# First weight pair of a split feed-forward block: all products with the first tokens before those with the second, its sums on one engine, and out rows joined with norms

## Chip, cores and metric

One core of a Trainium2 chip runs the whole kernel. The metric is device time in microseconds (us), as the median of several runs. A profile of one execution comes beside it. Engines are TensorE (PE: matrix products and transposes), VectorE (DVE), ScalarE (ACT), GpSimd (POOL) and SyncE (SP, which only issues DMAs). Each engine works through its own queue in order; across engines they wait on semaphores.

## The reference, cut to what matters

```python
x = x + 0.5 * swiglu(x, ffn1_norm, w_gate1, w_up1, w_down1)
...                      # windowed attention and latent attention on rms(x)
x = x + concat(rms(o_a), rms(o_b)) @ w_out
x = x + 0.5 * swiglu(x, ffn2_norm, w_gate2, w_up2, w_down2)

def swiglu(x, g, w_gate, w_up, w_down):
    h = rms(x, g)        # x * rsqrt(mean(x*x) + 1e-6) * g
    return (silu(h @ w_gate) * (h @ w_up)) @ w_down
```

x is 1024 tokens by 1024 features in float32; the hidden width is 2816, that is 22 tiles of 128.

## The kernel before, in words

Every float32 product is made from three products of rounded parts: an operand is split into `hi` (rounded by ACT, line 99 or, in `unit`, 358) and `lo` (the rest, subtracted by DVE, line 100 or 359), and `products` issues hi x hi, hi x lo and lo x hi (lines 120, 121, 122). A weight or activation is thus usable only when ACT and then DVE have treated it.

`ffn` runs twice, for the first and the last line of the reference. Its normed rows (`ys`, by `norm_rows`) are turned on PE (`bank`, line 226) and put as hi and lo into four blocks (`Block.put`, lines 212 and 213): B11 and B21 hold the two feature halves of the first 512 tokens, B12 and B22 those of the last 512. From the second hidden tile pair on, gate and up are made by a fast scheme with seven products in place of eight: it needs sums of the activation blocks (T1 to T4, made once by the generator `sums`, lines 235 to 255: `whole` adds hi and lo again, the rest subtracts) and sums S1 to S4 of each weight pair (`make`, line 295, called through `prepare`, which runs `AHEAD` = 5 products ahead). The first pair of hidden tiles (`f` = 0, 1, each with gate `wg` and up `wu`) is made plainly, while T1 to T4 are made: `half_unit(w, th)` multiplies one weight tile with the tokens of one half (`th`), 24 matmuls of 512 columns. So the first stage has eight half units: gate and up, two tiles, two halves. `finish` (lines 339 to 352) multiplies silu(gate) with up, writes it out on POOL's DMA queue and forms four sums of a finished pair.

Before the second `ffn`, `out_rows(1, t)` makes the second half of w_out's product for 128 tokens (24 matmuls; line 1212 adds it to x on DVE), the row is normed, and POOL's queue writes it to `x2`.

What sets the order of the work is a scheduler that takes the program as it is written and interleaves it per engine; which buffer becomes free when is set by pools (45 `slot`, 12 `tmp`, 8 PSUM banks).

Of the kernel before, what the change touches and what calls it, by code (L numbers as in the profile page):

```python
# [10 lines left out]
F32 = mybir.dt.float32  # L11
F32R = mybir.dt.float32r
AF = mybir.ActivationFunctionType
ALU = mybir.AluOpType
# [4 lines left out]
P = 128  # L19
# [40 lines left out]
def tile_layer(ctx: ExitStack, tc: tile.TileContext, x, g1n, mixn, g2n, wg1, wu1, wd1, wg2, wu2, wd2,  # L60
# [154 lines left out]
        def hi_lo(self, k):  # L215
            return tuple(self.t[hl][k // 2][:, k % 2, :] for hl in range(2))

    def ffn(rows_in, ys, gain, wg, wu, wd, act_d, xsrc, done, aside=iter(())):


        y = {}
# [6 lines left out]

        B11, B12, B21, B22, T1, T2, T3, T4 = (Block() for _ in range(8))

        def whole(blk, k, eng):

            d = tmp([P, 512])
            hi, lo = blk.hi_lo(k)
            eng.tensor_tensor(d, hi.bitcast(F32), lo.bitcast(F32), op=ALU.add)
            return d

        def turned(blk, th, k):
# [2 lines left out]

        def sums():
            for k in range(4):
                b12 = whole(B12, k, nc.gpsimd)
                t1 = whole(B11, k, nc.vector)
                nc.vector.tensor_tensor(t1, b12, t1, op=ALU.subtract)
                T1.put(k, t1)
                yield
                t3 = whole(B22, k, nc.gpsimd)
                nc.vector.tensor_tensor(t1, t3, t1, op=ALU.subtract)  # L250
                nc.vector.tensor_tensor(t3, t3, b12, op=ALU.subtract)
                T3.put(k, t3)
                yield
                t4 = whole(B21, k, nc.gpsimd)
                nc.gpsimd.tensor_tensor(t4, t4, t1, op=ALU.subtract)
                T2.put(k, t1)
                yield
                T4.put(k, t4)
                yield
# [25 lines left out]
        def make(c, nme, which):  # L285
            if which == "M11":
                load_pair(*((c, "u") if nme == "g" else (c + 1, "g")))
            f1, f2 = raws[(c, nme)]
            m = {"M11": f1[:, :512], "M12": f1[:, 512:], "M21": f2[:, :512], "M22": f2[:, 512:]}
            need = {"S1": ("M21", "M22", ALU.add), "S2": ("S1", "M11", ALU.subtract),  # L290
                    "S3": ("M11", "M21", ALU.subtract), "S4": ("M12", "S2", ALU.subtract)}
            if which in need:
                a_, b_, op = need[which]
                src = tmp([P, 512])
                nc.gpsimd.tensor_tensor(src, sums_[a_] if a_ in sums_ else m[a_], sums_[b_] if b_ in sums_ else m[b_],
                                        op=op)
# [33 lines left out]
        def finish(f, th, gate, up):  # L330
# [24 lines left out]
        def unit(raw, eng):  # L355
            hi, lo = slot([P, 1024], F32R), slot([P, 1024], F32R)
            for c in (slice(0, 512), slice(512, 1024)):
                nc.scalar.activation(hi[:, c], raw[:, c], AF.Copy)  # L358
                eng.tensor_tensor(lo[:, c], raw[:, c], hi[:, c].bitcast(F32), op=ALU.subtract)  # L359
# [12 lines left out]
        w0 = unit(first[0], nc.vector)  # L372
        for blk in (B11, B21):
            for k in range(4):
                turned(blk, 0, k)
        gen2 = sums()
        for f in range(2):
            for th in range(2):
                pts = []
                for i in range(2):  # L380
                    pts.append(half_unit(w1 if i else w0, th))
                    if f == 0 and th == 0 and i == 1:
                        for k in range(4):
                            turned(B12, 1, k)
                        for k in range(4):
                            turned(B22, 1, k)
                    if f == 0 and th == 0 and i == 0:
                        w1 = unit(first[1], nc.gpsimd)
                        for t in range(4, 8):
                            y[t] = ys(t)  # L390
                    if (f, th) > (0, 0):
                        for _ in range(3):
                            next(gen2, None)
                    if f == 0 and th == 1:
                        if i == 0:
                            n0 = unit(second[0], nc.vector)
                        else:
                            n1 = unit(second[1], nc.vector)
                    if f == 1 and th == 0 and i == 0:
                        load_pair(1, "g")  # L400
                    if f == 1 and th == 1:
                        prepare(1 + i)
                sg = tmp([P, 512])
                nc.scalar.activation(sg, pts[0], AF.Silu)
                finish(f, th, sg, pts[1])
            w0, w1 = (n0, n1) if f == 0 else (None, None)
            first = second = None if f else second
        for _ in gen2:
            pass
        B12.t = None  # L410


# [229 lines left out]

        defer(2 if t < 4 else 4, turn)

    ffn(load_rows, lambda t: norm_rows(x0.pop(t), both=True), g1n, wg1, wu1, wd1, act_d, x, mid, rel_bias_rows())


    def project(hT, ws, width, sink, ahead, last):
# [643 lines left out]

    ffn(lambda t: None, lambda t: normed[t], g2n, wg2, wu2, wd2, act_d, x2, fin)
    flush()


# [74 lines left out]
```

## Time and profile before

| | |
|---|---|
| median of 3 runs | 1884.24 us (1882.35 to 1884.5) |
| profiled execution | 1881.59 us, its span 1879.8 us |
| PE busy | 1825.7 us, 97% |
| DVE, ACT, POOL busy | 1271.2, 775.4, 627.8 us |
| mean granted clock of PE | 0.993 of full |

The span runs from the first to the last instruction. A page of the profile gives busy time by engine, by line and in slices; a timeline gives the rows in order of time as "start, duration, engine, line, operation, output <- inputs, count", with the idle time before a row and what ended it in brackets. The first `ffn` fills the span up to some 650 us, the second begins at 1221 us.

### The profile page before, as it was taken

To read this page: it belongs to the slowest core of one execution; us is meant where nothing else is said; L and a number is where in the kernel's file an instruction comes from. 1 tells how busy PE (TensorE), PEld (TensorE's weight loads), DVE (VectorE), ACT (ScalarE), POOL (GpSimd) and SP (SyncE) were. 2 spreads that over 40 slices of the span, in tenths; PEclk is the share of its full clock that TensorE was granted. 3 is DMA by queue.
4 is the path that set the end of the run, shared out by engine and by line. 5 is a ranking of instruction groups with operands and counts; after the bars stand their busy time and mean duration, and the time that the engine had idled before them with its cause. 6 is when DMAs were issued, how large, how long until landed. Compare 5 with 4: busy or idle time off the path is not lost.

```text
span 1879.8 us, 25149 instructions
## 1 busy us (share of the span) xinstructions
PE 1825.7 (97%) x9088; PEld 1546.2 (82%) x9088; DVE 1271.2 (68%) x2127; ACT 775.4 (41%) x1782; POOL 627.8 (33%) x706
## 2 busy tenths in 40 slices
PE   7899999999999999999998999979999999999998
PEld 5688888888888888888998888868888888888887
DVE  7976766766968363337888683388676767678681
ACT  5333333334445242236876582243333333253550
POOL 5643455442000122332454521256445444510000
PEclk9899999999999999999999999989999999999999
DMA  4223243326943231123311232313224222397422
GB/s 179 79 90 109 95 142 122 102 78 244 343 140 107 96 128 34 34 69 112 91 37 29 57 114 78 124 56 107 96 84 135 96 99 92 105 337 269 123 62 90
DMA packets 87078, 215.50 MB, mean 115 GB/s; under 512 B 11847, under 2 KB 17689, under 8 KB 86953
## 3 DMA queue, kind: packets, MB, share of 16 engines
q1 hardware_dynamic: 69608, 154.54, 25.0%
q0 software_dynamic: 17344, 59.35, 9.3%
q8 instruction: 71, 1.16, 0.2%
q14 instruction: 55, 0.44, 0.1%
HBM read 150.32 MB, written 59.33 MB: 112 GB/s over the span
## 4 chain that ended last, share of the span: by engine, by line
PE 88%; DVE 7%; issue 2%; DMA 1%; ACT 1%; POOL 1%; SPq 0%; POOLq 0%; DVEq 0%
PE ps L122 19%; PE ps L120 19%; PE ps L121 19%; PE ps L469 7%; PE ps L468 7%; PE ps L467 7%; PE ps L781 2%; DVE slot L100 2%; PE ps L807 2%; PE ps L755 1%; PE ps L846 1%; PE ps L771 1%; PE ps L969 1%; DVE slot L213 1%; PE ps L173 1%
## 5 line engine op out<-in xcount | busy, mean ns | idle before, releaser
L120 PE MATMUL ps<-slot,slot 128*128 128x512 f32 (+3 forms) x1728 | 664.3, 386 | 8.3 <-ACT slot L358 5.4
L122 PE MATMUL ps<-slot,slot 128*128 128x512 f32 (+3 forms) x1728 | 655.2, 383 | 14.4 <-DVE slot L359 13.1
L121 PE MATMUL ps<-slot,slot 128*128 128x512 f32 (+3 forms) x1728 | 661.5, 383 | 0.0
L122 PEld LDWEIGHTS ps<-slot,slot 128*128 128x128 f32 x1728 | 326.0, 189 | 78.3 <-DVE slot L359 14.0
L120 PEld LDWEIGHTS ps<-slot,slot 128*128 128x128 f32 x1728 | 325.8, 189 | 72.8 <-ACT slot L358 6.2
L121 PEld LDWEIGHTS ps<-slot,slot 128*128 128x128 f32 x1728 | 325.9, 189 | 62.3 <-DVE slot L213 0.5
L100 DVE TENSOR_TENSOR slot<-tmp,slot 128x512 fp32r<-128x512 f32 x346 | 332.5, 963 | 61.1 <-ACT slot L99 61.1
L99 ACT ACTIVATE slot<-tmp 128x512 fp32r<-128x512 f32 x346 | 215.2, 625 | 201.9 <-PE ps L469 43.6
L100 DVE TENSOR_TENSOR slot<-slot,slot 128x512 fp32r<-128x512 f32 (+3 forms) x312 | 254.2, 825 | 25.1 <-ACT slot L99 23.7
L468 PE MATMUL ps<-slot,slot 128*128 128x512 f32 x616 | 239.9, 390 | 0.0
L469 PE MATMUL ps<-slot,slot 128*128 128x512 f32 x616 | 239.7, 389 | 0.0
L467 PE MATMUL ps<-slot,slot 128*128 128x512 f32 x616 | 237.3, 389 | 0.0
L99 ACT ACTIVATE slot<-slot 128x512 fp32r<-128x512 f32 (+3 forms) x312 | 195.5, 641 | 61.0 <-PE ps L469 39.0
L468 PEld LDWEIGHTS ps<-slot,slot 128*128 128x128 f32 x616 | 115.6, 188 | 24.1
L469 PEld LDWEIGHTS ps<-slot,slot 128*128 128x128 f32 x616 | 115.6, 188 | 24.0
L467 PEld LDWEIGHTS ps<-slot,slot 128*128 128x128 f32 x616 | 115.6, 188 | 23.8
L543 ACT ACTIVATE tmp<-tmp 128x512 f32<-128x512 f32 x80 | 50.0, 625 | 199.6 <-DVE tmp L536 108.4
L528 DVE TENSOR_TENSOR tmp<-tmp,ps 128x512 f32<-128x512 f32 x40 | 27.5, 687 | 153.3 <-ACT tmp L527 153.3
L527 ACT ACTIVATE tmp<-ps 128x512 f32<-128x512 f32 x40 | 23.9, 597 | 226.1 <-PE ps L122 226.1
L342 POOL DMA_DIRECT2D act<-slot x22 | 16.2, 734 | 252.1 <-DVE slot L339 252.1
L475 DVE SCALAR_TENSOR_TENSOR slot<-ps,slot 128x512 f32<-128x512 f32 x56 | 36.9, 685 | 79.6 <-PE ps L469 79.5
L763 ACT ACTIVATE slot<-slot,tmp 128x256 f32<-128x256 f32 (+1 forms) x128 | 59.8, 468 | 22.4 <-DVE tmp L756 21.9
(174 smaller groups left out, 2278.2 us busy)
## 6 DMA issues: line engine op xcount, KB each, us to landing
tmp<-act SPq DMA_DIRECT2D x154, 256.0 KB
act<-slot POOLq DMA_DIRECT2D x66, 512.0 KB, 4.3
slot<-in_wg_dram SPq DMA_DIRECT2D x44, 512.0 KB
slot<-in_wu_dram SPq DMA_DIRECT2D x44, 512.0 KB
slot<-in_wd_dram SPq DMA_DIRECT2D x40, 512.0 KB
slot<-in_x_dram SPq DMA_DIRECT2D x16, 512.0 KB
x_mid<-slot POOLq DMA_DIRECT2D x16, 512.0 KB, 3.0
slot<-x_mid SPq DMA_DIRECT2D x16, 512.0 KB
```

The source lines that it names most:

```text
L99: nc.scalar.activation(hi, src, AF.Copy)
L100: nc.vector.tensor_tensor(lo, src, hi.bitcast(F32), op=ALU.subtract)
L120: nc.tensor.matmul(pt, ah, bh, start=first and i == 0, stop=False, skip_group_check=not first)
L121: nc.tensor.matmul(pt, ah, bl, start=False, stop=False, skip_group_check=not first)
L122: nc.tensor.matmul(pt, al, bh, start=False, stop=i == total - 1, skip_group_check=not first)
L467: nc.tensor.matmul(banks[i], ah, w[:, 0, :], start=first and k == 0, stop=False, skip_group_check=not first)
L468: nc.tensor.matmul(banks[i], ah, w[:, 1, :], start=False, stop=False, skip_group_check=not first)
L469: nc.tensor.matmul(banks[i], al, w[:, 0, :], start=False, stop=k == KD - 1, skip_group_check=not first)
L543: nc.scalar.activation(q, q, AF.Silu)
L763: nc.scalar.activation(self.p[:, e, :w], self.p[:, e, :w], AF.Exp, bias=self.m[e], scale=-1.0, accum_out=self.den[e])
L781: nc.tensor.matmul(po[:, e * HD:(e + 1) * HD], self.pt[:, n * P:(n + 1) * P], self.head["values"](self.far, self.j, e, j - nb + 1), start= ...
L807: nc.tensor.matmul(pt[:, :max(w, 256)], a, b, start=i == 0, stop=i == len(mats) - 1)
```

## The change

The loops over `f` (hidden tile) and `th` (token half) of the first stage are exchanged: all four half units with the first tokens are made first, then the four with the second. For that, four weight tiles are split and kept, and they are loaded before the rows of tokens 4 to 7. `sums` is advanced by four steps behind each half unit of the second tokens, instead of three behind each half unit from the third on. All additions that POOL made in `whole`, `sums`, `make`, `finish` and `unit` are on DVE. A new argument `lead` says how many rows of the second half are prepared ahead of the first half unit. In the second block (`lead` = 2) `out_rows`, `norm_rows` and the write to `x2` of a row group stand together in `last_rows`, which `ffn` calls, so that the out rows of groups 6 and 7 come behind the first half unit in the program.

```diff
         def sums():
             for k in range(4):
-                b12 = whole(B12, k, nc.gpsimd)
-                t1 = whole(B11, k, nc.vector)
+                t1, b12 = whole(B11, k), whole(B12, k)
 ...
-                t4 = whole(B21, k, nc.gpsimd)
-                nc.gpsimd.tensor_tensor(t4, t4, t1, op=ALU.subtract)
+                t4 = whole(B21, k)
+                nc.vector.tensor_tensor(t4, t4, t1, op=ALU.subtract)
@@ make
-                nc.gpsimd.tensor_tensor(src, sums_[a_] ...
+                nc.vector.tensor_tensor(src, sums_[a_] ...
@@ finish
-                nc.gpsimd.tensor_tensor(s43[:, 1, :], a11, a21, op=ALU.subtract)
-                nc.gpsimd.tensor_tensor(s43[:, 0, :], a12, s12[:, 1, :], op=ALU.subtract)
+                nc.vector.tensor_tensor(s43[:, 1, :], a11, a21, op=ALU.subtract)
+                nc.vector.tensor_tensor(s43[:, 0, :], a12, s12[:, 1, :], op=ALU.subtract)
@@ the first stage
-        first = [raw_of(wg[0]), raw_of(wu[0])]
+        raw = [raw_of(w[f]) for f in range(2) for w in (wg, wu)]
         for t in range(4, 8):
             rows_in(t)
-        second = [raw_of(wg[1]), raw_of(wu[1])]
-        for t in range(4):
+        for t in range(4 + lead):
             y[t] = ys(t)
 ...
-        for f in range(2):
-            for th in range(2):
+        for th in range(2):
+            for f in range(2):
                 pts = []
                 for i in range(2):
+                    n = 2 * f + i
+                    if th == 0 and raw:
+                        w.append(unit(raw.pop(0)))
+                    if th == 0 and n == 3:
+                        for blk in (B12, B22):
+                            for k in range(4):
+                                turned(blk, 1, k)
+                    pts.append(half_unit(w[n], th))
+                    if th == 0 and n == 0:
+                        for t in range(4 + lead, 8):
+                            y[t] = ys(t)
+                    if th == 1:
+                        w[n] = None
+                        if n == 0:
+                            load_pair(1, "g")
+                        if n >= 2:
+                            prepare(n - 1)
+                        for _ in range(4):
+                            next(sums, None)
@@ ahead of the second block
-    normed = {}
-    for t in range(NT):
+    def last_rows(t):
         out_rows(1, t)
-        normed[t] = norm_rows(xs[t])
-        nc.gpsimd.dma_start(x2[t * P:(t + 1) * P, :], xs[t])
+        y = norm_rows(xs[t])
+        nc.gpsimd.dma_start(x2[t * P:(t + 1) * P, :], xs.pop(t))
+        return y
```

How the queues change. Numbers behind names are buffers of the program; some lines count one to six lower or higher in the changed program (`whole` is line 236, the out rows' addition 1206, and `unit` now calls `split`, line 100). DVE in the first block, before: what stands ahead of the split of the third weight tile (slot_107 to slot_443); lines 246 to 251 and 235 are `sums`, slots 424 to 439 are T blocks.

```order
L250 TENSOR_TENSOR tmp_420<-tmp_427,tmp_420 128x512
L246 TENSOR_TENSOR tmp_479<-tmp_477,tmp_479 128x512
L251 TENSOR_TENSOR tmp_427<-tmp_427,tmp_418 128x512
L100 TENSOR_TENSOR slot_424<-tmp_479,slot_423 128x512
L100 TENSOR_TENSOR slot_432<-tmp_427,slot_431 128x512
L250 TENSOR_TENSOR tmp_479<-tmp_484,tmp_479 128x512
L100 TENSOR_TENSOR slot_439<-tmp_420,slot_438 128x512
L235 TENSOR_TENSOR tmp_534<-slot_182,slot_183 128x512
L251 TENSOR_TENSOR tmp_484<-tmp_484,tmp_477 128x512
L359 TENSOR_TENSOR slot_443<-slot_107,slot_442 128x512 x2
```

DVE at the same weight tile now (slot_99 to slot_301; the fourth is slot_101 to slot_336; L193 is the last row's norm, L236 `whole`, L213 the second tokens' blocks).

```order
L100 TENSOR_TENSOR slot_301<-slot_99,slot_300 128x512 x2
L339 TENSOR_TENSOR slot_333<-tmp_331,ps_306 128x512
L193 TENSOR_SCALAR slot_290<-slot_109,small_295 128x512 x2
L100 TENSOR_TENSOR slot_336<-slot_101,slot_335 128x512 x2
L236 TENSOR_TENSOR tmp_488<-slot_166,slot_167 128x512
L213 SCALAR_TENSOR_TENSOR slot_372<-ps_366,small_85,slot_371 128x512
L213 SCALAR_TENSOR_TENSOR slot_372<-ps_375,small_85,slot_371 128x512
L236 TENSOR_TENSOR tmp_490<-slot_371,slot_372 128x512
```

The splits of the third and fourth tile have moved ahead of every sum but none of the sums is gone. They stand later, up to the low half of the weight of pair 1's product M12 (slot_649), on DVE:

```order
L251 TENSOR_TENSOR tmp_605<-tmp_605,tmp_598 128x512
L255 TENSOR_TENSOR tmp_613<-tmp_613,tmp_596 128x512
L100 TENSOR_TENSOR slot_602<-tmp_652,slot_601 128x512
L295 TENSOR_TENSOR tmp_742<-slot_484,tmp_697 128x512
L100 TENSOR_TENSOR slot_610<-tmp_605,slot_609 128x512
L250 TENSOR_TENSOR tmp_652<-tmp_659,tmp_652 128x512
L100 TENSOR_TENSOR slot_617<-tmp_596,slot_616 128x512
L100 TENSOR_TENSOR slot_621<-tmp_613,slot_620 128x512
L347 TENSOR_TENSOR slot_677<-slot_457,slot_333 128x512
L349 TENSOR_TENSOR slot_678<-slot_333,slot_457 128x512
L295 TENSOR_TENSOR tmp_774<-slot_591 128x512
L100 TENSOR_TENSOR slot_649<-slot_484,slot_649 128x512
```

From the first L213 of the part above to this last row there are 62 instructions, eight of them L213; L255, L295 and L349 were POOL's. In the second block the same stretch has 65.

PE at pair 1, before: M11 ends (ps_685) and M12 (ps_686) follows whole.

```order
L121 MATMUL ps_685<-slot_183,slot_639 128x512
L122 MATMUL ps_685<-slot_182,slot_639 128x512
L120 MATMUL ps_686<-slot_198,slot_669 128x512
L121 MATMUL ps_686<-slot_199,slot_669 128x512
L122 MATMUL ps_686<-slot_198,slot_669 128x512
L120 MATMUL ps_686<-slot_198,slot_669 128x512
```

PE there now: behind M12's first matmul (L120, not shown) stand the hi products of five more products, and only then M12's third, which needs the low half.

```order
L121 MATMUL ps_686<-slot_199,slot_649 128x512
L120 MATMUL ps_740<-slot_493,slot_689 128x512
L121 MATMUL ps_740<-slot_494,slot_689 128x512
L120 MATMUL ps_741<-slot_501,slot_694 128x512
L121 MATMUL ps_741<-slot_502,slot_694 128x512
L120 MATMUL ps_685<-slot_508,slot_699 128x512
L121 MATMUL ps_685<-slot_509,slot_699 128x512
L120 MATMUL ps_797<-slot_166,slot_706 128x512
L121 MATMUL ps_797<-slot_167,slot_706 128x512
L120 MATMUL ps_798<-slot_198,slot_721 128x512
L121 MATMUL ps_798<-slot_199,slot_721 128x512
L122 MATMUL ps_686<-slot_198,slot_649 128x512
```

Twelve matmuls of six products have moved ahead of the first one that needs a low half of these weights.

More of the change, by code (lines that the diff above doesn't have):

```diff
@@ L216, in hi_lo, with ffn @@
             return tuple(self.t[hl][k // 2][:, k % 2, :] for hl in range(2))
-    def ffn(rows_in, ys, gain, wg, wu, wd, act_d, xsrc, done, aside=iter(())):
+    def ffn(rows_in, ys, gain, wg, wu, wd, act_d, xsrc, done, lead, aside=iter(())):
         y = {}
@@ L229, in ffn, with whole @@
         B11, B12, B21, B22, T1, T2, T3, T4 = (Block() for _ in range(8))
-        def whole(blk, k, eng):
+        def whole(blk, k):
             d = tmp([P, 512])
             hi, lo = blk.hi_lo(k)
-            eng.tensor_tensor(d, hi.bitcast(F32), lo.bitcast(F32), op=ALU.add)
+            nc.vector.tensor_tensor(d, hi.bitcast(F32), lo.bitcast(F32), op=ALU.add)
             return d
@@ L248, in sums @@
                 yield
-                t3 = whole(B22, k, nc.gpsimd)
+                t3 = whole(B22, k)
                 nc.vector.tensor_tensor(t1, t3, t1, op=ALU.subtract)
@@ L294, in make @@
                 src = tmp([P, 512])
-                nc.gpsimd.tensor_tensor(src, sums_[a_] if a_ in sums_ else m[a_], sums_[b_] if b_ in sums_ else m[b_],
+                nc.vector.tensor_tensor(src, sums_[a_] if a_ in sums_ else m[a_], sums_[b_] if b_ in sums_ else m[b_],
                                         op=op)
@@ L353, in finish, with unit @@
                 del acts[c]
-        def unit(raw, eng):
+        def unit(raw):
             hi, lo = slot([P, 1024], F32R), slot([P, 1024], F32R)
             for c in (slice(0, 512), slice(512, 1024)):
-                nc.scalar.activation(hi[:, c], raw[:, c], AF.Copy)
-                eng.tensor_tensor(lo[:, c], raw[:, c], hi[:, c].bitcast(F32), op=ALU.subtract)
+                split(hi[:, c], lo[:, c], raw[:, c])
             return hi, lo
@@ L365, in ffn @@
         nc.sync.dma_start(gcol, gain)
-        first = [raw_of(wg[0]), raw_of(wu[0])]
+        raw = [raw_of(w[f]) for f in range(2) for w in (wg, wu)]
         for t in range(4, 8):
             rows_in(t)
-        second = [raw_of(wg[1]), raw_of(wu[1])]
-        for t in range(4):
+        for t in range(4 + lead):
             y[t] = ys(t)
-        w0 = unit(first[0], nc.vector)
+        w = [unit(raw.pop(0))]
         for blk in (B11, B21):
@@ L375, in ffn @@
                 turned(blk, 0, k)
-        gen2 = sums()
-        for f in range(2):
-            for th in range(2):
+        sums = sums()
+        for th in range(2):
+            for f in range(2):
                 pts = []
                 for i in range(2):
[L381 to L389, printed above, removed]
-                            y[t] = ys(t)
[L391 to L402, printed above, removed]
+                    n = 2 * f + i
[8 more added lines that the diff above has]
+                        for t in range(4 + lead, 8):
+                            y[t] = ys(t)
+                    if th == 1:
[6 more added lines that the diff above has]
+                            next(sums, None)
                 sg = tmp([P, 512])
@@ L405, in ffn @@
                 finish(f, th, sg, pts[1])
[L406 to L409, printed above, removed]
+        y.clear()
         B12.t = None
@@ L643, in mid @@
         defer(2 if t < 4 else 4, turn)
-    ffn(load_rows, lambda t: norm_rows(x0.pop(t), both=True), g1n, wg1, wu1, wd1, act_d, x, mid, rel_bias_rows())
+    ffn(load_rows, lambda t: norm_rows(x0.pop(t), both=True), g1n, wg1, wu1, wd1, act_d, x, mid, 0, rel_bias_rows())
     def project(hT, ws, width, sink, ahead, last):
@@ L1282, in tile_layer @@
     x2 = dram.tile([S, D], F32, name="x_mid2")
-    normed = {}
-    for t in range(NT):
+    def last_rows(t):
         out_rows(1, t)
-        normed[t] = norm_rows(xs[t])
-        nc.gpsimd.dma_start(x2[t * P:(t + 1) * P, :], xs[t])
+        y = norm_rows(xs[t])
+        nc.gpsimd.dma_start(x2[t * P:(t + 1) * P, :], xs.pop(t))
+        return y
     def fin(t, xt):
         nc.sync.dma_start(out[t * P:(t + 1) * P, :], xt)
-    ffn(lambda t: None, lambda t: normed[t], g2n, wg2, wu2, wd2, act_d, x2, fin)
+    ffn(lambda t: None, last_rows, g2n, wg2, wu2, wd2, act_d, x2, fin, 2)
     flush()
```

## The prediction

> **What bounds the kernel now.** I read the page first: engines, then the costliest groups.
>
> ```profile
> span 1879.8 us, 25149 instructions
> PE 1825.7 (97%) x9088; PEld 1546.2 (82%) x9088; DVE 1271.2 (68%) x2127; ACT 775.4 (41%) x1782; POOL 627.8 (33%) x706
> ```
>
> TensorE (PE) is the bound: 54 us of the span are without a matmul. An edit that touches no matmul can give time only where PE waits or runs at a lower clock. Second view: who PE waited for (columns: total us, times, longest).
>
> ```profile
> PE ps L122 <- DVE slot L359: 13.1, 2, 7.1
> PE ps L120 <- ACT slot L358: 5.4, 2, 2.9
> ```
>
> L358 and L359 are the two halves of `unit()`, the weight split. Each wait came twice, once per feed-forward block (FFN). Third view: the timeline of PE in the first stage of each block; the bracket is idle time before the row.
>
> ```profile
> 14.32 0.50 PE L120 MATMUL ps<-slot,slot 128*128 128x512 f32 x1 [0.80 <-DVE slot L213]
> 25.34 2.45 PE L226 MATMUL ps<-ident,slot 128*128 128x128 f32 x21
> 28.04 0.98 PE L226 MATMUL ps<-ident,slot 128*128 128x128 f32 x7 [0.24 <-DVE slot L193]
> 29.93 0.66 PE L226 MATMUL ps<-ident,slot 128*128 128x128 f32 x4 [0.91 <-DVE slot L213]
> 44.98 0.50 PE L120 MATMUL ps<-slot,slot 128*128 128x512 f32 x1 [2.88 <-ACT slot L358]
> 52.85 0.79 PE L122 MATMUL ps<-slot,slot 128*128 128x512 f32 x1 [7.14 <-DVE slot L359]
> 57.10 0.39 PE L120 MATMUL ps<-slot,slot 128*128 128x512 f32 x1
> 84.00 0.50 PE L122 MATMUL ps<-slot,slot 128*128 128x512 f32 x1 [1.30 <-DVE slot L100]
> ...
> 1226.26 0.50 PE L120 MATMUL ps<-slot,slot 128*128 128x512 f32 x1 [1.04 <-DVE slot L213]
> 1254.38 0.50 PE L120 MATMUL ps<-slot,slot 128*128 128x512 f32 x1 [2.47 <-ACT slot L358]
> 1261.10 0.80 PE L122 MATMUL ps<-slot,slot 128*128 128x512 f32 x1 [5.96 <-DVE slot L359]
> 1265.38 0.39 PE L120 MATMUL ps<-slot,slot 128*128 128x512 f32 x1
> ```
>
> From 14.32 to 25.34 PE ran two half units, 48 matmuls, in 11.02 us: 0.230 us each, 5.5 us a half unit. A transpose costs 2.45/21 = 0.117 us. From 52.85 to 57.10 ten matmuls took 4.25 us where ten cost 2.30: the clock was halved, 2.0 us lost. In the second block 4.28 us, again 2.0. What PE lost: first block 0.24 + 0.91 + 2.88 + 7.14 + 1.30 + 2.0 = 14.5 us, second 1.04 + 2.47 + 5.96 + 2.0 = 11.5 us. **Together 26.0 us; more cannot be won here.**
>
> Why is the split late? The timelines of VectorE (DVE) and GpSimd (POOL):
>
> ```profile
> 42.63 6.75 POOL L235 TENSOR_TENSOR tmp<-slot,slot 128x512 f32<-128x512 f32 x4
> ...
> 43.14 3.44 DVE L100 TENSOR_TENSOR slot<-tmp,slot 128x512 fp32r<-128x512 f32 x2
> 46.51 1.74 DVE L250 TENSOR_TENSOR tmp<-tmp,tmp 128x512 f32<-128x512 f32 x1
> 52.12 1.28 DVE L359 TENSOR_TENSOR slot<-slot,slot 128x512 fp32r<-128x512 f32 x2
> 57.53 1.28 DVE L100 TENSOR_TENSOR slot<-tmp,slot 128x512 fp32r<-128x512 f32 x2
> 58.74 0.68 DVE L250 TENSOR_TENSOR tmp<-tmp,tmp 128x512 f32<-128x512 f32 x1
> 59.45 0.69 DVE L251 TENSOR_TENSOR tmp<-tmp,tmp 128x512 f32<-128x512 f32 x1
> ```
>
> While POOL adds, each DVE addition takes about 1.74 us; from 52.12, with POOL idle, two take 1.28, and the 12 from there to 59.45 take 7.33: 0.61 us each. The split of the second weight pair stands in DVE's queue behind ten such slowed sums.
>
> **The change, part by part.**
>
> *Order: all four half units with the first tokens, then four with the second.* No matmul is added. The third and fourth units are split before any sum, directly behind the norms of the second tokens. Whether that is early enough is read from these rows:
>
> ```profile
> 12.79 4.74 ACT L212 ACTIVATE slot<-ps,small 128x512 fp32r<-128x512 f32 x8 [1.93 <-PE ps L226]
> 17.37 1.20 ACT L358 ACTIVATE slot<-slot 128x512 fp32r<-128x512 f32 x2
> 18.41 0.68 ACT L186 ACTIVATE slot<-slot 128x512 f32<-128x512 f32 x1
> 19.20 1.28 ACT L404 ACT_TABLE_LOAD   x1
> 20.55 0.60 ACT L404 ACTIVATE tmp<-ps 128x512 f32<-128x512 f32 x1
> ...
> 13.51 5.36 DVE L213 SCALAR_TENSOR_TENSOR slot<-ps,small,slot 128x512 fp32r<-128x512 f32 x8 [0.77 <-ACT slot L212]
> 24.25 0.87 DVE L193 TENSOR_SCALAR slot<-slot,small 128x512 f32<-128x512 f32 x2
> ```
>
> ACT keeps its order up to the silu at 20.55, does three more squares at 0.6 and the new split of two halves at 1.2: 24.2. DVE is through with the first tokens at 18.9 and has four L100 at 0.61, four squares at 0.7 and three L193 pairs at 0.8 ahead: 7.6 us, to 26.5. PE takes up the third unit at 25.3 with hi products and then 18 transposes (2.1 us), so it asks for the low half at 27.9. The 10.02 us of split waits and their 2.0 go; so do 0.24 and 0.91, the transposes now standing where their rows are long normed. In the second block the same 8.43 and 2.0 go.
>
> *Loads.* On SP's queue the second pair of weights now passes x rows 4 to 7. All twelve transfers were through by 20 before:
>
> ```profile
> 15.00:20.00 5.00, 5.00 (x24) 4.12 (x23) 4.54 (x8) 4.98 (x10) 1.87 (x2) 1.00 0.60 226
> 20.00:25.00 5.00, 5.00 (x24) 4.14 (x23) 4.01 (x10) 2.91 (x8) 3.52 (x9) 1.00 0.01 3
> ```
>
> (last column GB/s). The first of those rows is used near 19, the last near 24: cost 0, at most 1 if the second row lands only at 20 plus.
>
> *Out rows with norms, second block.* The out rows of tokens 6 and 7 (48 matmuls) move behind the first transposes and lie inside and behind the first half unit; PE does the same work. They now cover the evacuation of the transposes, so 1.04 goes. POOL's writes of x move with them and are read only in the down stage: 0.
>
> *Sums on VectorE alone.* This is what takes a part back. Before, POOL did three `whole` and one subtraction per `k`, the second split, and two of the four sums of a finished pair. All these now queue on DVE, and a wait appears one stage later, ahead of pair 1's second product (M12). I count in DVE's queue, with the rows above. First block: the third half unit ends at 14.32 + 3 x 5.5 + 18 x 0.117 = 32.9. ACT then does silu (0.6) and the first of the second tokens' evacuations (0.7): DVE starts L213 at 34.3. From there to the low half of M12's weight stand 62 instructions: 8 L213 at 0.67 (5.36/8) and 54 at 0.61: 38.3 us, to 72.6. PE comes at 14.32 + 8 x 5.5 + 32 x 0.117 = 62.1, does M11 (12 matmuls, 2.75) and the 12 matmuls of six products that the new order puts ahead of M12's third one: 67.6. **New wait: 5.0 us.** ACT's splits for these twelve are queued behind the same sums, so the wait comes in pieces: some 3 before them, the rest behind. After it DVE has three more halves to give, each ahead of PE's need by over 0.5 us.
>
> Second block, same sum from its own rows:
>
> ```profile
> 1210.88 0.69 DVE L1212 TENSOR_TENSOR slot<-ps,slot 128x512 f32<-128x512 f32 x1 [1.52 <-PE ps L122]
> 1221.56 3.65 PE L226 MATMUL ps<-ident,slot 128*128 128x128 f32 x32
> ```
>
> Out row 5 ends at 1210.7. Transposes 3.7; three half units and the two out rows, 120 matmuls, 27.6: 1242.0. Transposes and five half units: 1273.2; M11 and the 12: 1278.7. DVE starts L213 at 1242.0 + 0.2 + 0.6 + 0.7 = 1243.5, has 8 and 57: 5.4 + 34.8, to 1283.7. **New wait: 5.0 us.**
>
> Bounds of the new wait: none if DVE had kept up (0); at the addition rate of the disturbed stretch (1.74) far over what it replaces. I take 0.61, because no POOL addition is left near it; the rows from 52.12 on are the nearest. A 0.1 us pause where an instruction needs the one just before (58.74 to 59.45 is 0.71 instead of 0.61) may add 0.5 to 2 us per block.
>
> *Steady stage.* Ten sums per pair of weight tiles (eight L295, two of `finish`) move to DVE.
>
> ```profile
> 100.00:200.00 100.00, 100.00 (x443) 82.84 (x442) 68.88 (x81) 31.79 (x58) 39.91 (x32) 1.00 0.28 96
> ...
> L100 DVE TENSOR_TENSOR slot<-tmp,slot 128x512 fp32r<-128x512 f32 x62 | 67.9, 1095 | 13.7 <-ACT slot L99 13.7
> ```
>
> PE is busy throughout there (second number), DVE 69%. A pair lasts about 37.5 us and will need 40 DVE instructions x 0.61 = 24 us, 65%, as the L100 of 1095 ns goes back to 680. PE has no wait there, so nothing is won; I cost it at 0. What covers it is products split five ahead.
>
> **Sum.** 26.0 won, 5.0 + 5.0 given back: 16.0. The profiled execution took 1881.59 us (span 1879.8): 1865.6. The median of the runs, 1884.24, is 2.65 above it, so 1868.2 in its terms: 1868.
>
> **The clock in the new wait.** Row of PEclk (the number after POOL's) around the old wait and in a thin stretch:
>
> ```profile
> 45.00:46.00 1.00, 0.71 (x2) 0.27 (x2) 1.00 (x1) 0.93 (x2) 1.00 (x2) 1.00 0.71 287
> 47.00:48.00 1.00, 0.00 (x0) 0.00 (x0) 1.00 (x1) 0.00 (x0) 1.00 (x2) 0.50 0.00 0
> 1004.00:1006.00 2.00, 0.87 (x8) 0.63 (x7) 2.00 (x7) 2.00 (x11) 1.01 (x4) 1.00 0.00 0
> 1006.00:1008.00 2.00, 0.64 (x6) 0.67 (x7) 2.00 (x8) 1.23 (x3) 1.46 (x3) 1.00 0.00 0
> ```
>
> It fell after some 4 us with two matmuls and held at 38% busy over 4 us. The new wait comes in pieces (3 us idle, 3.3 mostly busy, 1.5 idle), nearer to the thin stretch, so I leave the clock at full in the sum. [...]
>
> **Rivals.**
> 1. *The clock falls in both new waits.* Price as before, 2.0 each: 1872; with pauses as above up to 1876. For it: 3 us idle is close to the 2.88 and 2.47 that began the old falls. Against: 12 matmuls follow at once, not two.
> 2. *No wait remains*, DVE keeps up: 1858. For it: DVE stands idle about 4 us before its L213s. Against: the order puts only one sum there.
> 3. *The waits only move.* If the additions average 0.61 + 8/62 = 0.74 us, all 16 are gone: 1884. For it: 1.74 and 1095 ns above. Against: every slowed row lies beside a POOL addition, and none is left.
> 4. *Slower: the steady stage.* DVE works in order; an addition that waits for PE's sums now holds the weight sums behind it, which POOL made independently. From 0.8 us per pair, 20 pairs, the gain is gone; at the 1.30 us of the row at 84.00 it is 26 us: 1894. For it: two thirds busy in order. Against: after pair 1's first addition that waits, the order leaves some 5 us until PE needs the weight behind it.
>
> **How the numbers follow.** Forecast (1862 to 1872) 0.66; clock or pauses (to 1876) 0.13; no wait (1856 to 1861) 0.09; moved (1877 to 1887) 0.06; slower, steady 0.06. From 1860 to 1876 holds a little over eight in ten. About 0.2% (3.8 us) is what can be told from no change: faster 0.89, same 0.05, slower 0.06.
>
> **What would show it.** PE's waits for the split of the second pair gone in both blocks; no POOL addition left and DVE additions at 0.68 us in the first stage; PE waiting for ACT L99 and DVE L100 near 65 to 73 and 1266 to 1274, about 5 us in each; pair 1's first product of the first block near 62; PE without waits from 100 to 600. The prediction is wrong if the new wait is over 10 us or missing, if DVE additions stay over 0.74, or if PE waits appear in the steady stage.

## The result, and the profile after

The changed kernel took 1868.01 us (median of four runs, 1863.59 to 1868.51), the kernel before 1884.01 beside it: a ratio of 0.9911, 95% interval 0.9894 to 0.9929. Measured again later, 1866.70 us and 0.9907 (0.9893 to 0.992). The forecast was 1868, range 1860 to 1876. The number came out; the experiments show that the reason given for it was half wrong.

The profiled execution after took 1863.59 us. Its engines, and what PE waited for (columns: total us, times, longest):

```profile
span 1861.8 us, 25005 instructions
PE 1823.7 (98%) x9088; PEld 1546.4 (83%) x9088; DVE 1228.4 (66%) x2367; ACT 777.7 (42%) x1782; POOL 273.0 (15%) x466
...
PE ps L120 <- ACT slot L99: 6.1, 2, 3.3
```

DVE runs 240 instructions more in 43 us less. In the first stages POOL makes no 128x512 addition any more. The two waits for the weight split of the second pair (13.1 and 5.4 us in sum) are gone, and a wait for L99 has come. The timeline of PE in the first stages shows where (bracket: idle time before the row):

```profile
14.76 0.50 PE L120 MATMUL ps<-slot,slot 128*128 128x512 f32 x1 [0.77 <-DVE slot L213]
35.51 0.49 PE L120 MATMUL ps<-slot,slot 128*128 128x512 f32 x1 [0.52 <-DVE slot L213]
65.36 0.39 PE L122 MATMUL ps<-slot,slot 128*128 128x512 f32 x1
68.50 0.80 PE L120 MATMUL ps<-slot,slot 128*128 128x512 f32 x1 [2.76 <-ACT slot L99]
73.79 0.63 PE L122 MATMUL ps<-slot,slot 128*128 128x512 f32 x1
...
1266.96 0.79 PE L120 MATMUL ps<-slot,slot 128*128 128x512 f32 x1 [3.33 <-ACT slot L99]
```

The last matmul of pair 1's first product (M11) starts at 65.36; M12's hi products begin at 68.50, its third product only at 73.79. What PE waits for is in DVE's timeline and windows (busy us of PE, PEld, DVE, ACT, POOL; then PE's granted clock, DMA share, GB/s):

```profile
34.71 1.41 DVE L213 SCALAR_TENSOR_TENSOR slot<-ps,small,slot 128x512 fp32r<-128x512 f32 x2 [2.90 <-ACT slot L212]
41.19 3.69 DVE L236 TENSOR_TENSOR tmp<-slot,slot 128x512 f32<-128x512 f32 x6
71.88 0.68 DVE L100 TENSOR_TENSOR slot<-slot,slot 128x512 fp32r<-128x512 f32 x1
...
34.60:72.56 37.96, 34.68 (x146) 28.04 (x145) 37.85 (x63) 17.99 (x33) 1.52 (x2) 0.94 0.14 50
...
67.00:68.00 1.00, 0.00 (x0) 0.00 (x0) 1.00 (x3) 1.00 (x3) 0.00 (x0) 0.88 0.70 266
68.00:69.00 1.00, 0.50 (x1) 0.50 (x2) 1.00 (x3) 1.00 (x3) 0.00 (x0) 0.50 0.00 0
...
100.00:200.00 100.00, 100.00 (x442) 82.80 (x442) 66.10 (x109) 32.42 (x57) 8.13 (x12) 1.00 0.28 99
```

From the second tokens' first evacuation to the low half of M12's weight DVE is busy for 37.85 of 37.96 us: that queue sets the end of the stage. The clock fell to 0.50 in the wait. In the steady stage PE stays full (100.00 of 100 us).

**A ruler for the stages.** Single executions differ in the middle of the program, which the change doesn't touch, so I measure each block apart: from the first half unit to the first matmul of the down products (first block), and from the first addition of the out rows to the last down matmul (second block). The rows give first and last start of a line; before and after:

```profile
L467 PE MATMUL ps<-slot,slot x616: 387/389/482, 454.8 to 1874.2; 128*128 128x512 f32 x154
L1212 DVE TENSOR_TENSOR slot<-ps,slot x16: 681/692/692, 1135.7 to 1221.8; 128x512 f32<-128x512 f32 x16
...
L461 PE MATMUL ps<-slot,slot x616: 388/389/477, 445.8 to 1856.6; 128*128 128x512 f32 x154
L1206 DVE TENSOR_TENSOR slot<-ps,slot x16: 684/692/692, 1124.3 to 1219.4; 128x512 f32<-128x512 f32 x16
```

Before, 454.8 - 14.32 = 440.5 and 1874.2 - 1135.7 = 738.5; after, 431.0 and 732.3. The same readings of every kernel, in us, with the median time and the ratio to the kernel before:

| kernel | block 1 | block 2 | both, against before | median | ratio (95%) |
|---|---|---|---|---|---|
| before | 440.5 | 738.5 | 0 | 1884.0 | 1 |
| changed | 431.0 | 732.3 | -15.7 | 1868.0 | 0.9911 (0.9894-0.9929) |
| changed, again (e9) | 430.9 | 732.2 | -15.9 | 1866.7 | 0.9907 (0.9893-0.992) |
| e1 new order, sums on POOL | 442.0 | 742.1 | +5.1 | 1889.2 | 1.0029 (1.0018-1.0039) |
| e2 old order, sums on DVE | 433.9 | 730.6 | -14.5 | 1870.1 | 0.9926 (0.991-0.9943) |
| e3 out rows first | 430.0 | 732.3 | -16.7 | 1866.9 | 0.9912 (0.9897-0.9927) |
| e4 pair sums on POOL | 433.8 | 734.9 | -10.3 | 1871.6 | 0.9937 (0.9921-0.9953) |
| e5 e2 with early split | 429.5 | 727.4 | -22.1 | 1861.0 | 0.9881 (0.9866-0.9896) |
| e6 up products early | 428.8 | 729.5 | -20.7 | 1860.7 | 0.9888 (0.9872-0.9905) |
| e7 sums from high halves | 425.3 | 726.0 | -27.7 | 1856.6 | 0.9858 (0.9843-0.9872) |
| e8 filler matmuls | 429.8 | 731.1 | -18.1 | 1867.1 | 0.9917 (0.9902-0.9932) |
| e10 early transposes | 429.9 | 728.9 | -20.2 | 1864.0 | 0.9891 (0.9878-0.9905) |
| e11 e6 and e10 together | 427.0 | 726.1 | -25.9 | 1857.0 | 0.9859 (0.9846-0.9872) |
| e12 old order, early split and up products | 431.3 | 731.2 | -16.5 | 1864.2 | 0.9904 (0.9891-0.9918) |

e1 to e4, e5 to e8 and e9 to e12 ran together. Each stage is one reading; the two of the changed kernel agree to 0.1 us (together -15.8 below). But e3, whose first block is the changed kernel's, reads 430.0 there, 1.0 less: at pair 1 its clock was halved for 3.41 us and the changed kernel's for 6.83. So a difference of 1 us in a block can be the clock's alone; where one as small is argued from, the rows stand beside it.

### The profile page after: what moved, and what is told of

Its sections match the earlier page's. It is cut to its first block, busy times and chain, and to the rows that moved or that the text cites. A ratio compares the mean times of both kernels' runs of the same rounds, so it can differ in the third digit from the quotient of the medians.

```text
span 1861.8 us, 25005 instructions
## 1 busy us (share of the span) xinstructions
PE 1823.7 (98%) x9088; PEld 1546.4 (83%) x9088; DVE 1228.4 (66%) x2367; ACT 777.7 (42%) x1782; POOL 273.0 (15%) x466
## 4 chain that ended last, share of the span: by engine, by line
PE 92%; DVE 3%; ACT 2%; DMA 1%; issue 1%; POOL 1%; SPq 0%; POOLq 0%; ACTq 0%
PE ps L120 20%; PE ps L121 20%; PE ps L122 20%; PE ps L462 7%; PE ps L463 7%; PE ps L461 7%; PE ps L775 2%; PE ps L801 2%; PE ps L749 1%; PE ps L840 1%; PE ps L765 1%; PE ps L227 1%; PE ps L963 1%; ACT slot L99 1%; PE ps L173 1%
## 5 line engine op out<-in xcount | busy, mean ns | idle before, releaser
L120 PE MATMUL ps<-slot,slot 128*128 128x512 f32 (+3 forms) x1728 | 666.4, 387 | 8.5 <-ACT slot L99 6.1
L122 PE MATMUL ps<-slot,slot 128*128 128x512 f32 (+3 forms) x1728 | 647.2, 383 | 0.0
L120 PEld LDWEIGHTS ps<-slot,slot 128*128 128x128 f32 x1728 | 326.6, 189 | 72.7 <-ACT slot L99 6.9
L122 PEld LDWEIGHTS ps<-slot,slot 128*128 128x128 f32 x1728 | 325.0, 188 | 62.6
L99 ACT ACTIVATE slot<-tmp 128x512 fp32r<-128x512 f32 x346 | 214.5, 625 | 269.7 <-DVE tmp L295 133.0
L100 DVE TENSOR_TENSOR slot<-tmp,slot 128x512 fp32r<-128x512 f32 x346 | 235.7, 685 | 27.7 <-ACT slot L99 21.8
L100 DVE TENSOR_TENSOR slot<-slot,slot 128x512 fp32r<-128x512 f32 (+3 forms) x328 | 228.6, 708 | 27.7 <-ACT slot L99 26.2
L99 ACT ACTIVATE slot<-slot 128x512 fp32r<-128x512 f32 (+3 forms) x328 | 205.1, 641 | 66.7 <-PE ps L463 43.1
L530 DVE TENSOR_TENSOR tmp<-tmp,ps 128x512 f32<-128x512 f32 x40 | 27.5, 688 | 126.3 <-PE ps L122 126.3
L522 DVE TENSOR_TENSOR tmp<-tmp,ps 128x512 f32<-128x512 f32 x40 | 27.5, 688 | 108.4 <-ACT tmp L521 104.6
L342 POOL DMA_DIRECT2D act<-slot x22 | 15.7, 715 | 469.2 <-DVE slot L339 469.2
```

What stands on the lines that cost most here:

```text
L99: nc.scalar.activation(hi, src, AF.Copy)
L100: nc.vector.tensor_tensor(lo, src, hi.bitcast(F32), op=ALU.subtract)
L120: nc.tensor.matmul(pt, ah, bh, start=first and i == 0, stop=False, skip_group_check=not first)
L122: nc.tensor.matmul(pt, al, bh, start=False, stop=i == total - 1, skip_group_check=not first)
```

## The experiments

### One part of the change alone (e1, e2)

The new order, with the sums put back on POOL (the splits of the weights stay on DVE):

```diff
-                t1, b12 = whole(B11, k), whole(B12, k)
+                b12 = whole(B12, k, nc.gpsimd)
+                t1 = whole(B11, k)
...
-                t3 = whole(B22, k)
+                t3 = whole(B22, k, nc.gpsimd)
...
-                nc.vector.tensor_tensor(t4, t4, t1, op=ALU.subtract)
+                nc.gpsimd.tensor_tensor(t4, t4, t1, op=ALU.subtract)
...                                  # also in make() and finish()
```

> The new order of the half units, with the sums on GpSimd (POOL) as before the change: three wholes and one subtraction per k, the S sums of a pair, two of the four sums of finish. The unit splits stay on VectorE (DVE). My theory: the split of the second pair is in time (its waits of 7.14 and 5.96 us stay away), but the sums, beside which each DVE addition takes 1.74 us in place of 0.61, are not through when PE comes to pair 1 near 62 us; PE waits 10 to 20 us per block for them, and most or all of the gain is lost: 1876 to 1896. Rival: the order alone is the gain, and POOL's share would have relieved DVE: 1868 or below, with a wait at pair 1 of at most 5 us per block.

Measured: 1889.21 us, slower than before (ratio 1.0029, interval above 1). PE's waits in its timeline, and DVE beside POOL:

```profile
64.92 0.50 PE L122 MATMUL ps<-slot,slot 128*128 128x512 f32 x1 [1.54 <-DVE slot L100]
74.73 0.80 PE L120 MATMUL ps<-slot,slot 128*128 128x512 f32 x1 [7.22 <-ACT slot L99]
78.71 0.79 PE L122 MATMUL ps<-slot,slot 128*128 128x512 f32 x1 [2.75 <-DVE slot L100]
85.90 0.50 PE L122 MATMUL ps<-slot,slot 128*128 128x512 f32 x1 [2.28 <-DVE slot L100]
...
39.96 7.64 POOL L236 TENSOR_TENSOR tmp<-slot,slot 128x512 f32<-128x512 f32 x5 [3.21 <-DVE slot L213]
46.37 1.78 DVE L251 TENSOR_TENSOR tmp<-tmp,tmp 128x512 f32<-128x512 f32 x1
66.59 0.68 DVE L251 TENSOR_TENSOR tmp<-tmp,tmp 128x512 f32<-128x512 f32 x1
67.42 1.58 POOL L256 TENSOR_TENSOR tmp<-tmp,tmp 128x512 f32<-128x512 f32 x1 [3.70 <-DVE tmp L251]
```

The split waits are gone, and in the first block 13.8 us of waits at pair 1 stand in their place, as the theory said. The same subtraction (L251) takes 1.78 us beside POOL's run of additions (39.96 to 47.60) and 0.68 us within the 3.70 us in which POOL is idle, up to 67.42.

The old order, with every addition on DVE:

```diff
-                b12 = whole(B12, k, nc.gpsimd)
+                b12 = whole(B12, k, nc.vector)
                 t1 = whole(B11, k, nc.vector)
...                                  # so in the other sums, make(), finish()
-                        w1 = unit(first[1], nc.gpsimd)
+                        w1 = unit(first[1], nc.vector)
```

> The order of before, with all additions and both splits of weights on VectorE. My theory: additions fall to 0.61 us, but the split of the second pair still stands in DVE's queue behind the sums of the first tokens, now some 13 of them and not 10, so a wait of 3 to 8 us per block stays ahead of the second pair and a smaller one follows at pair 1: 1872 to 1882. Rival A: sums on DVE are the whole gain, 1868 or below. Rival B: sums on DVE bring nothing without the order, 1884 or above.

Measured: 1870.08 us, under my range and 2 us over rival A's time. In the stages it wins 14.5 of the 15.8 us:

```profile
47.21 0.79 PE L120 MATMUL ps<-slot,slot 128*128 128x512 f32 x1 [4.43 <-ACT slot L358]
48.77 0.79 PE L120 MATMUL ps<-slot,slot 128*128 128x512 f32 x1 [0.34 <-ACT slot L358]
...
1249.76 0.50 PE L120 MATMUL ps<-slot,slot 128*128 128x512 f32 x1 [0.75 <-ACT slot L358]
1251.32 0.50 PE L120 MATMUL ps<-slot,slot 128*128 128x512 f32 x1 [0.82 <-ACT slot L358]
1253.73 0.51 PE L122 MATMUL ps<-slot,slot 128*128 128x512 f32 x1 [0.75 <-DVE slot L359]
```

The split still stands behind sums, but the waits fell from 10.02 and 8.43 to 4.77 and 2.32 us, the halved clock is gone from the second block (matmuls start 0.23 us apart there), and no wait follows at pair 1, against my theory. So the two parts are not a gain and its price: the order alone costs 5.1 us, DVE alone wins 14.5, both win 15.8.

### The smaller parts (e3, e4)

The changed kernel, with all out rows ahead of the second block again:

```diff
-    def last_rows(t):
+    normed = {}
+    for t in range(NT):
         out_rows(1, t)
-        y = norm_rows(xs[t])
-        nc.gpsimd.dma_start(x2[t * P:(t + 1) * P, :], xs.pop(t))
-        return y
+        normed[t] = norm_rows(xs[t])
+        nc.gpsimd.dma_start(x2[t * P:(t + 1) * P, :], xs[t])
```

> The changed kernel, but with all eight out rows and norms ahead of the second block's first stage, as before the change. My theory: the wait of 1.04 us for the evacuation of the transposes returns, the rest stays: 1868 to 1870, not to be told from the changed kernel. Rival: the move of the out rows is part of the gain by the place that the norms take on DVE and ScalarE: 1872 or more.

Measured: 1866.92 us, 1 under my range; block 2 takes 732.3 us, as in the changed kernel. The wait of 1.04 us came back. The rows of pair 1 here, and (last two) in the changed kernel; L100 makes the low half of M12's weight, and L122 is M12's third product:

```profile
1217.74 0.50 PE L120 MATMUL ps<-slot,slot 128*128 128x512 f32 x1 [1.04 <-DVE slot L213]
1270.63 0.79 PE L120 MATMUL ps<-slot,slot 128*128 128x512 f32 x1 [2.76 <-ACT slot L99]
1274.48 0.69 DVE L100 TENSOR_TENSOR slot<-slot,slot 128x512 fp32r<-128x512 f32 x1
1275.22 0.50 PE L122 MATMUL ps<-slot,slot 128*128 128x512 f32 x1 [0.20 <-DVE slot L100]
...
1270.43 0.68 DVE L100 TENSOR_TENSOR slot<-slot,slot 128x512 fp32r<-128x512 f32 x1
1272.25 0.59 PE L122 MATMUL ps<-slot,slot 128*128 128x512 f32 x1
```

Counted from the first addition of the out rows, DVE is through with that low half after 148.0 us here (1275.17 - 1127.2) and after 146.8 us in the changed kernel (1271.11 - 1124.3). So the move of the out rows wins 1.2 us on DVE. The time doesn't show it: the clock was halved for 6.83 us at pair 1 in the changed kernel and for 3.41 here, so there PE takes up M12's third product only 1.1 us after the low half is done, again at 148.0. That the move is worth nothing is thus not shown.

In the changed kernel, the sums of a weight pair and two of finish's four on POOL:

```diff
-                nc.vector.tensor_tensor(src, sums_[a_] if a_ in sums_ else m[a_], ...
+                nc.gpsimd.tensor_tensor(src, sums_[a_] if a_ in sums_ else m[a_], ...
...
-                nc.vector.tensor_tensor(s43[:, 1, :], a11, a21, op=ALU.subtract)
-                nc.vector.tensor_tensor(s43[:, 0, :], a12, s12[:, 1, :], op=ALU.subtract)
+                nc.gpsimd.tensor_tensor(s43[:, 1, :], a11, a21, op=ALU.subtract)
+                nc.gpsimd.tensor_tensor(s43[:, 0, :], a12, s12[:, 1, :], op=ALU.subtract)
```

> The changed kernel, but the S sums of a weight pair and two of the four sums of finish on GpSimd as before; the wholes and the subtraction of the first stage stay on DVE. My theory: from pair 2 on PE waits for nothing whichever engine adds, so the placement is worth nothing there, and the end of the first stage loses what POOL's additions slow on DVE, 1 to 3 us per block beside some 8 additions fewer in DVE's queue (5 us): 1866 to 1872. Rival (the steady stage matters): 0.3 us or more per pair in 20 pairs, 6 us either way: below 1863 or above 1874.

Measured: 1871.64 us; 2.8 us more in block 1 and 2.7 in block 2 than the changed kernel. In the steady stage PE has no idle time either way, while DVE does 78 instructions in more time than the changed kernel's 109:

```profile
100.00:200.00 100.00, 100.00 (x443) 82.83 (x442) 68.65 (x78) 30.48 (x55) 43.74 (x37) 1.00 0.29 100
```

So these sums matter at the end of the first stage alone, and there DVE is better off doing them itself.

### What bounds the stage (e5 to e8)

My new theory was that DVE's queue as a whole is the bound, wherever the split stands. The kernel of e2, with the second pair's split ahead of the sums:

```diff
+                        n0, n1 = unit(second[0], nc.vector), unit(second[1], nc.vector)
                     if f == 0 and th == 0 and i == 0:
                         w1 = unit(first[1], nc.vector)
...
-                    if f == 0 and th == 1:
-                        if i == 0:
-                            n0 = unit(second[0], nc.vector)
-                        else:
-                            n1 = unit(second[1], nc.vector)
```

> The order of before with all additions on VectorE (as in the kernel that does this alone), but the split of the second weight pair ahead of all sums. My new theory: what bounds the first stage is DVE's queue as a whole, so a wait that is taken from the split comes back at pair 1, where the S sums are late: waits for L358 and L359 gone (4.8 us in the first block, 2.3 in the second), 2 to 4 us of waits for L99 and L100 in their place, 1865 to 1870. Rival: the order of the half units is not needed at all, the place of the split alone is enough: 1862 or below, with less than 1 us of waits per block.

Measured: 1860.98 us, the rival's time: the order of the half units isn't needed. Its waits are not quite the rival's: for L99 and L100 2.11 us stay in the first block, where the rival allowed 1 and my theory 2 to 4, and none in the second. All that PE still waits for after the first half unit, and DVE's first evacuation of the second tokens:

```profile
30.62 0.66 PE L226 MATMUL ps<-ident,slot 128*128 128x128 f32 x4 [0.91 <-DVE slot L213]
65.13 0.50 PE L120 MATMUL ps<-slot,slot 128*128 128x512 f32 x1 [0.65 <-ACT slot L99]
67.74 0.50 PE L120 MATMUL ps<-slot,slot 128*128 128x512 f32 x1 [0.31 <-DVE slot L100]
70.15 0.50 PE L122 MATMUL ps<-slot,slot 128*128 128x512 f32 x1 [1.15 <-DVE slot L100]
1218.67 0.50 PE L120 MATMUL ps<-slot,slot 128*128 128x512 f32 x1 [1.04 <-DVE slot L213]
...
29.81 1.41 DVE L213 SCALAR_TENSOR_TENSOR slot<-ps,small,slot 128x512 fp32r<-128x512 f32 x2 [0.75 <-ACT slot L212]
```

L213 starts at 29.81, in the changed kernel at 34.71: the new order turns the second tokens a half unit later, and all sums with them.

The changed kernel, with pair 1's up products M11 and M12 ahead of the products that need sums:

```diff
             order += [(c, "g", w) for w in ("M11", "M12")]
+            if c == 1:
+                order += [(c, "u", w) for w in ("M11", "M12")]
+                order += [(c, "g", w) for w in ("S1", "S3", "S2", "S4", "M22")]
+                order += [(c, "u", w) for w in ("S1", "S3", "S2")]
+                continue
...
-                            prepare(n - 1)
+                            prepare(2 * n - 2)
...                                  # and start(c, "u") ahead of middle(c, "g") for c == 1
```

> The changed kernel, with pair 1's up products M11 and M12 ahead of its gate products of sums: 24 matmuls, 5.5 us, that need no sum. If the new wait (2.76 and 3.33 us in the first piece, some 2 to 3 behind it, and the halved clock) comes from DVE's queue being late by about 5 us at pair 1 alone, the waits for L99 and L100 fall under 1.5 us per block: 1858 to 1862. Rival (DVE's queue bounds, the wait only moves on to the products of sums): 1865 to 1869.

Measured: 1860.72 us, in the theory's range, though waits of 2.84 and 2.56 us stay where under 1.5 was expected.

The changed kernel, with 16 additions fewer per block. It leaves the low halves out of the sums, so it only shows what the queue costs and can't replace the kernel:

```diff
-                t1, b12 = whole(B11, k), whole(B12, k)
-                nc.vector.tensor_tensor(t1, b12, t1, op=ALU.subtract)
+                h11, h12, h21, h22 = (b.hi_lo(k)[0].bitcast(F32) for b in (B11, B12, B21, B22))
+                t1 = tmp([P, 512])
+                nc.vector.tensor_tensor(t1, h12, h11, op=ALU.subtract)
```

> The changed kernel, with the sums of token blocks made from the high halves alone: the low halves are left out of the sums, and with them 16 additions per block on DVE, 9.8 us at 0.61. If DVE's queue is the bound of the first stage, the new wait goes with them: no wait for L99 or L100 at pair 1, 1856 to 1860. Rival: the wait has another cause (ScalarE's halves, the loads) and stays: 1866 to 1869.

Measured: 1856.55 us, and no wait of PE at pair 1 in either block. With 9.8 us less in DVE's queue the new wait is gone: DVE is its cause.

The price of the clock:

```diff
             product(A, c, nme, "M11", B11)
+            if c == 1 and nme == "g":
+                fill = ps()
+                x_, y_ = B11.hi_lo(0)
+                for i in range(12):
+                    nc.tensor.matmul(fill, x_[:, :P], x_, start=i == 0, stop=i == 12 - 1)
```

> The changed kernel, with 12 matmuls without use (2.75 us) behind pair 1's first product, in the new wait. The prediction's price of the clock was 2.0 us per block; by the trace of the changed kernel it cost 0.8 to 1.2, since the halved matmuls lie in the wait for DVE's low half. If so, the clock stays at full here, and the time is 1866 to 1868; by the price of 2.0 it is 1864 or below. If 12 matmuls don't keep the clock up, 1868 to 1870.

Measured: 1867.12 us; the clock stayed at full in both first stages (M12's hi products start 0.23 to 0.29 us apart, 0.34 behind a wait, where the changed kernel has 0.43). M12's third product starts at

```profile
73.15 0.50 PE L122 MATMUL ps<-slot,slot 128*128 128x512 f32 x1 [0.56 <-DVE slot L100]
```

in place of 73.79, though this execution's first half unit starts 0.39 us later (15.15 against 14.76), and the stages are 2.3 us shorter together: some 1.1 per block is what the clock cost in the changed kernel. The time can't tell 2 us; the stages and the clock can.

### The cause in the new order, and a better kernel (e9 to e12)

> The changed kernel again, as it is, beside the three below: 1866 to 1869, for a comparison on the same chip at the same time.

Measured: 1866.70 us. Beside it, the transposes a half unit earlier:

```diff
-                    if th == 0 and n == 3:
+                    if th == 0 and n == 2:
                         for blk in (B12, B22):
```

> The changed kernel with the transposes of the second tokens one half unit earlier: ahead of the third half unit in place of the fourth. Theory: the new wait at pair 1 has its cause in the new order itself; the first evacuation of the second tokens on DVE starts at 34.7 us there and at 29.8 in the kernel with the old order and the early split, so all sums start 4.9 us later. Transposed earlier, DVE starts its L213 near 30, and of the new wait (2.76 and 3.33 us, some 3 behind each) at most 1.5 us per block is left: 1859 to 1863. Rival: DVE's queue is full from its first addition to pair 1 anyway, the start doesn't matter: 1866 to 1869.

Measured: 1864.04 us, 1 over the theory's range. In the stages 4.4 us are won against the changed kernel, less than e5 (6.3) or e7 (11.9) win:

```profile
29.66 1.49 PE L227 MATMUL ps<-ident,slot 128*128 128x128 f32 x11 [0.92 <-DVE slot L339]
32.31 0.50 PE L120 MATMUL ps<-slot,slot 128*128 128x512 f32 x1 [1.17 <-DVE slot L213]
69.19 0.50 PE L120 MATMUL ps<-slot,slot 128*128 128x512 f32 x1 [1.21 <-ACT slot L99]
73.27 0.50 PE L122 MATMUL ps<-slot,slot 128*128 128x512 f32 x1 [0.74 <-DVE slot L100]
...
28.92 0.68 DVE L339 TENSOR_TENSOR slot<-tmp,ps 128x512 f32<-128x512 f32 x1
29.52 0.88 DVE L193 TENSOR_SCALAR slot<-slot,small 128x512 f32<-128x512 f32 x2
31.52 5.35 DVE L213 SCALAR_TENSOR_TENSOR slot<-ps,small,slot 128x512 fp32r<-128x512 f32 x8
```

At pair 1 the wait fell from 2.76 and what followed it to 1.95 us. But PE now waits among the transposes (0.92) for L339, the product of `finish`, behind which the last row's norm (L193) still stands in DVE's queue, and then for their evacuation (1.17). I had counted neither. The later start of the sums is thus one cause of the new wait, not the whole.

Both cures (the edits of e6 and e10):

> Both cures of the changed kernel: the transposes of the second tokens a half unit earlier, and pair 1's up products M11 and M12 ahead of its products of sums. If each takes away the same wait, they don't add: 1857 to 1861, at most 3 us under the better of the two alone. If the waits are two different ones, 1854 or below.

Measured: 1856.97 us, against 1866.70 of the changed kernel in the same runs; no run of the one reaches the other's (1859.28 at most, 1865.28 at least). No wait of PE is left at pair 1. It beats both kernels and leaves nothing of the computation out. The cures take more than I allowed: 3.8 us under e6, measured at another time, and 5.2 in the stages. There they add: against the changed kernel e6 wins 4.9 us, e10 4.4, both 10.1.

The last kernel takes the old order with e5's split, e6's order of products without its `prepare` line, and the moved out rows:

> All that helped, on the order of before: all additions on VectorE, the split of the second weight pair ahead of the sums, pair 1's up products M11 and M12 first, the last two out rows inside the second block's first stage. Left of the waits of the early split alone (0.91, 0.65, 0.31 and 1.15 us in the first block, 1.04 in the second) would be the 0.91 and at most 1 more: 1857 to 1860. Rival: by moving the out rows, the second tokens are normed later and the sums start later: 1861 to 1865.

Measured: 1864.19 us, over my range, the rival's time. Not for the rival's reason: the wait is the same in the first block, which has no out rows.

```profile
68.46 0.50 PE L120 MATMUL ps<-slot,slot 128*128 128x512 f32 x1 [2.21 <-ACT slot L99]
1266.66 0.51 PE L120 MATMUL ps<-slot,slot 128*128 128x512 f32 x1 [2.19 <-ACT slot L99]
```

Besides the order of the half units, it differs from e6 and e11 in that the splits of the up products are not brought ahead in the queue with the products; that this is the cause was not tried.

## Why the prediction came out, point by point

- *PE bound, and 26.0 us lost in two places.* The place is right, the size low: e7 wins 27.7 us in the stages. Where the other 1.7 lie, no run shows.
- *The split waits and their clock go.* Right.
- *The new wait at pair 1, 5.0 us each.* Place and releaser are right, and the count of DVE's queue is good: the low half of M12's weight is done at 72.56, forecast 72.6, at 0.60 to 0.61 us for each addition. The price came out larger: M12's third product starts at 73.79, where PE without a wait would have begun it at 68.35 (65.36 and 13 matmuls of 0.23), so 5.4 us in the first block, behind the 0.52 at 35.51. The stages give 27.7 - 15.8 = 11.9 us given back in both, forecast 10.0; with the clock at full (e8) it is 27.7 - 18.1 = 9.6. So the wait was sized well, and the clock is what came on top.
- *The clock stays at full.* Wrong. It fell in both waits and stayed at 0.50 for 6.83 us each: the first rival's mechanism, to which I gave 0.13 with its pauses. Its price was also wrong, 1.1 us and not 2.0 (e8): the matmuls at half speed lay in the wait for DVE's low half. The clock is the term of the sum that was put at nothing, 2.3 us in both blocks. The two errors, 1.7 us too little lost before and 1.9 too little given back, cancel; that the sum of 16.0 meets the stages' 15.8 is luck by so much.
- *The out rows, 1.04 us won.* The wait goes, and DVE is through 1.2 us earlier at pair 1 (e3 against the changed kernel). In the executions that were profiled the longer halved clock took this back.
- *Loads and steady stage at 0.* Right: PE is busy for 100.00 of 100 us, and the first half unit starts at 14.26 to 15.15 in all runs, with no regard to the order.
- *"This is what takes a part back", of the sums on VectorE.* This is the step that failed. I gave the whole gain to the new order and a cost to DVE's sums. In the new order, sums on DVE win 20.9 us (e1 against the changed kernel); in the old, 14.5 (e2). And the order isn't needed: with the split ahead of the sums, the old order wins 22.1 us (e5). The row for it was quoted: a DVE addition took 1.74 us beside POOL's and 0.61 alone. I used it to say why the split was late, and did not recount the old queue at 0.61 with POOL's share added; e2 is that count.
- *The profiled execution.* It is 2 us under the 1865.6 forecast for it since the middle of the program, unchanged, took 678.5 us in place of 680.9; in the second execution it took 682.1.

## What to carry to other kernels

When a change has two parts, price each alone and both together before giving one the gain: here the new order alone loses 5.1 us and the engine's move wins 14.5. Where one queue is full up to the end of a stage, three things counted here: how fast it works beside its neighbours (in e1 the same subtraction took 1.78 us beside POOL's additions and 0.68 with POOL idle), when its first input comes, and what the waiting engine can do first. Look at the clock beside each reading: in e3 a difference of 3.41 us at half speed hid what an edit won. And a slowed instruction in a row was a price that also fell away (1.74 us to 0.61 here): recount the queue at the undisturbed rate.

## What the runs showed of the hardware

The clock falls in shorter waits than I had thought, and not in all of them. By the windows above it fell 2.0 us into the wait that began at 65.74 (68.50 less 2.76; in 67 to 68 the mean is 0.88, so at 0.50 for the last 0.24 us). In e6 (first row) a wait of 2.03 us did not bring it down, and in e12 it fell 1.0 us after PE had taken up work again, behind the wait of 2.21:

```profile
70.42 0.50 PE L120 MATMUL ps<-slot,slot 128*128 128x512 f32 x1 [2.03 <-ACT slot L99]
...
68.00:69.00 1.00, 0.54 (x2) 0.32 (x3) 1.00 (x3) 1.00 (x3) 0.00 (x0) 1.00 0.38 143
69.00:70.00 1.00, 1.00 (x4) 0.77 (x4) 1.00 (x3) 1.00 (x3) 0.00 (x0) 0.72 0.00 0
```

So the time from the start of a wait to the fall isn't one number: 2.0 us in the changed kernel and 3.2 in e12 (from 66.25, which is 68.46 less 2.21, to 69.44, since the mean of 0.72 in 69 to 70 is 0.56 us at 0.50). Why the wait in e6 left the clock up is not shown.

The stretches at 0.50 that end inside the profiled runs before and after lasted 3.41, 6.83 or 10.24 us: before from 46.63 to 56.87, 1056.97 to 1063.80 and 1254.95 to 1265.19, after from 67.76 to 74.58, 1047.38 to 1050.80 and 1265.84 to 1272.66. The falls in the changed kernel lie 979.63 and 218.45 us apart, 287 and 64 times the shortest stretch; whether that decides which wait brings the clock down was not tried by a run of its own.

The clock goes with much of the scatter of the middle part, which no edit touches. With one stretch of 3.41 us at 0.50 in it, it took 678.5 us (after), with one of 6.83, 680.9 (before). In the six runs whose first stages show no matmul at the halved clock, it took 679.3 us at a mean clock of 0.999 over the run (e6), 681.5 and 681.6 at 0.998 (e11, e8), 682.3 and 683.6 at 0.997 (e7, e10) and 683.5 at 0.996 (e5). Two executions of the changed kernel differ there by 3.6 us (678.5 and, in e9, 682.1), more than several of the edits above.
